# Batch normalization on one core: the first tile in one transfer, the four parameters as single rows from ScalarE's queue

## The chip, the core and the metric

The kernel runs on one core of a Trainium2 chip. The time is the device time of one execution in microseconds, from the program's start to its end; a kernel is run several times and the median is given. Beside it stands a profiled execution, from which all views below come.

## What is computed

```python
def reference(x, gamma, beta, running_mean, running_var):
    eps = 1e-5
    mean = running_mean.reshape(1, -1, 1, 1)
    ...
    return gamma * (x - mean) / np.sqrt(var + eps) + beta
```

`x` is 32 x 256 x 128 x 128 float32, 537 MB, and so is the output; the four parameters have 256 values each, one for each channel. Each value of `x` is multiplied by its channel's scale `gamma / sqrt(var + eps)`, and the channel's shift `beta - mean * scale` is added.

## The kernel before

**Tiles.** The 256 channels are two blocks of 128, one channel on each of the 128 partitions. One image and one block make a tile of 128 x 16384 values, 64 KB on each partition and 8.4 MB in all. There are 64 tiles (`NT`), and three buffers of that size (`NBUF`): tile `i` lies in buffer `i % 3`, is computed in place, and is stored from there.

**Loads (SP's queue).** The loop at L98 to L106 issues all loads in order of the tiles. The loads of tiles 1 and 2 wait for nothing. From tile 3 on, load `i` waits for two things: that the store of tile `i - 3`, which had the same buffer, has landed (L103), and that VectorE has done the first part of tile `i - 1` (L106), so that a load is issued just after the one before it has landed.

**The computation.** VectorE does a tile in two `tensor_scalar` instructions, columns 0 to 2560 and 2560 to 14336 (L160 to L162, through `vector_part`); the first of them waits for the tile's load. ScalarE does the last 2048 columns with one `activation` (`scalar_part`). The last tile is cut otherwise: ScalarE takes 7168 columns of it.

**Stores (ScalarE's queue).** In the loop at L163 to L168, ScalarE waits until both of VectorE's parts of tile `i` are done and until the store of tile `i - 1` has landed, does its own columns, and issues the store of the tile (`store`, L156). So there is at most one store under way at a time, and, from tile 3 on, at most one load.

**The start.** Tile 0 is an exception: it is loaded in two halves of 8192 columns, the left one at L90 with a semaphore of its own (`early`), the right one at L97. Between them stand the four parameters (L92 to L96), on the same queue. Each is read 16 times (`partition_broadcast(NE)`), 16 rows of 1 KB, into partitions 0 to 15 of a 32 x 1024 tile `rows`, which VectorE has set to zero before (L91); the first of the four transfers waits for that. All four count up one semaphore, `fetched`.

VectorE waits for `fetched`, transposes `rows` in blocks of 32 x 32 (L110), and copies the first column of each block to where it belongs (L115, four copies), so that each parameter then stands with one value on each partition. Only row 0 of `rows` is used by this. One square root on ScalarE (L117) and four small VectorE instructions (L124 to L127) make scale and shift. VectorE then does tile 0 in two parts, columns 0 to 8192 after `early` (L158) and 8192 to 14336 after the right half (L159).

Of the kernel before, what the change touches and what calls it, by code (L numbers as in the profile page):

```python
# [13 lines left out]
VCOLS = 14336  # L14
# [3 lines left out]
@with_exitstack  # L18
def kernel(
    ctx: ExitStack,  # L20
    tc: tile.TileContext,
    x: bass.AP,
    gamma: bass.AP,
    beta: bass.AP,
    running_mean: bass.AP,
    running_var: bass.AP,
    out: bass.AP,
):
    nc = tc.nc
    eps = 1e-5  # L30
    f32 = mybir.dt.float32

    N, C, H, W = x.shape
    P = nc.NUM_PARTITIONS
    assert C % P == 0
    NCB = C // P
    HW = H * W
    NT = N * NCB
    B = 32
    NQ = P // B  # L40
    NE = 16
    NPAR = 4

    xr = x.rearrange("n (cb p) h w -> (n cb) p (h w)", p=P)
    outr = out.rearrange("n (cb p) h w -> (n cb) p (h w)", p=P)

    params = ctx.enter_context(tc.tile_pool(name="params", bufs=1))
    data = ctx.enter_context(tc.tile_pool(name="data", bufs=1))
    params.tile([P, PAD], f32, name="pad", tag="pad")
    bufs = [data.tile([P, HW], f32, name=f"t{s}", tag=f"t{s}") for s in range(NBUF)]  # L50
    rows = params.tile([B, NPAR * C], f32, name="rows", tag="rows")
    turned = params.tile([B, NPAR * C], f32, name="turned", tag="turned")
    par = params.tile([P, NPAR, NCB], f32, name="par", tag="par")
    eps_t = params.tile([P, 1], f32, name="eps_t", tag="eps")
    std_t = params.tile([P, NCB], f32, name="std_t", tag="std")
    rstd_t = params.tile([P, NCB], f32, name="rstd_t", tag="rstd")
    scale_t = params.tile([P, NCB], f32, name="scale_t", tag="scale")
    ms_t = params.tile([P, NCB], f32, name="ms_t", tag="ms")
    shift_t = params.tile([P, NCB], f32, name="shift_t", tag="shift")

    loaded = [tc.alloc_semaphore(f"loaded{s}") for s in range(NBUF)]
    stored = [tc.alloc_semaphore(f"stored{s}") for s in range(NBUF)]
    early = tc.alloc_semaphore("early")
    vdone = tc.alloc_semaphore("vdone")
    adone = tc.alloc_semaphore("adone")
    fetched = tc.alloc_semaphore("fetched")
    vec = tc.alloc_semaphore("vec")
    act = tc.alloc_semaphore("act")  # L70

    with tc.tile_critical():  # L72
        count = [0]

        def step(inst, sem=None, value=None):

            if sem is not None:
                inst._wait_ge(sem, value)
            elif count[0]:
                inst._wait_ge(vec, count[0])  # L80
            inst.then_inc(vec, 1)
            count[0] += 1
            return count[0]

        left, right = slice(0, HW // 2), slice(HW // 2, HW)
        last = NT - 1

        nc.sync.dma_start(out=bufs[0][:, left], in_=xr[0][:, left]).then_inc(early, 16)  # L90
        zeroed = step(nc.vector.memset(rows[:], 0.0))  # L91
        for r, ap in enumerate((running_var, gamma, beta, running_mean)):  # L92
            inst = nc.sync.dma_start(out=rows[0:NE, r * C : (r + 1) * C], in_=ap.partition_broadcast(NE))  # L93
            if r == 0:
                inst._wait_ge(vec, zeroed)
            inst.then_inc(fetched, 16)  # L96
        nc.sync.dma_start(out=bufs[0][:, right], in_=xr[0][:, right]).then_inc(loaded[0], 16)  # L97
        for i in range(1, NT):  # L98
            s, turn = i % NBUF, i // NBUF


            if turn:
                nc.sync.wait_ge(stored[s], 16 * turn)  # L103
            inst = nc.sync.dma_start(out=bufs[s][:], in_=xr[i]).then_inc(loaded[s], 16)
            if turn:
                inst._wait_ge(vdone, 2 * (i - 1) + 1)  # L106


        step(nc.vector.memset(eps_t[:], eps))  # L109
        step(nc.vector.transpose(out=turned[:], in_=rows[:]), fetched, 16 * NPAR)  # L110

        blocks = turned.rearrange("p (rc q b) -> p rc q b", q=NQ, b=B)
        flat = par.rearrange("p r cb -> p (r cb)")
        for q in range(NQ):
            placed = step(nc.vector.tensor_copy(out=flat[q * B : (q + 1) * B], in_=blocks[:, :, q, 0]))  # L115
        var_t, gamma_t, beta_t, mean_t = (par[:, r] for r in range(NPAR))
        nc.scalar.activation(  # L117
            out=std_t[:],
            in_=var_t,
            func=mybir.ActivationFunctionType.Sqrt,  # L120
            bias=eps_t[:],
            scale=1.0,
        )._wait_ge(vec, placed).then_inc(act, 1)
        step(nc.vector.reciprocal(out=rstd_t[:], in_=std_t[:]), act, 1)  # L124
        step(nc.vector.tensor_mul(out=scale_t[:], in0=gamma_t, in1=rstd_t[:]))  # L125
        step(nc.vector.tensor_mul(out=ms_t[:], in0=mean_t, in1=scale_t[:]))  # L126
        ready = step(nc.vector.tensor_sub(out=shift_t[:], in0=beta_t, in1=ms_t[:]))  # L127
        nc.vector.wait_ge(vec, ready)

        def vector_part(i, first, end):  # L130
            t, cb = bufs[i % NBUF], i % NCB
            return nc.vector.tensor_scalar(  # L132
                out=t[:, first:end],
                in0=t[:, first:end],
                scalar1=scale_t[:, cb : cb + 1],
                scalar2=shift_t[:, cb : cb + 1],
                op0=mybir.AluOpType.mult,
                op1=mybir.AluOpType.add,
            ).then_inc(vdone, 1)

        def scalar_part(i, first):
            t, cb = bufs[i % NBUF], i % NCB
            return nc.scalar.activation(  # L143
                out=t[:, first:],
                in_=t[:, first:],
                func=mybir.ActivationFunctionType.Identity,
                bias=shift_t[:, cb : cb + 1],
                scale=scale_t[:, cb : cb + 1],
            ).then_inc(adone, 1)

        def landed(i):
            return loaded[i % NBUF], 16 * (i // NBUF + 1)

        def store(i):
            s = i % NBUF
            nc.scalar.dma_start(out=outr[i], in_=bufs[s][:])._wait_ge(adone, i + 1).then_inc(stored[s], 16)  # L156

        vector_part(0, 0, HW // 2)._wait_ge(early, 16)  # L158
        vector_part(0, HW // 2, VCOLS)._wait_ge(*landed(0))  # L159
        for i in range(1, NT):  # L160
            vector_part(i, 0, STEP)._wait_ge(*landed(i))
            vector_part(i, STEP, VLAST if i == last else VCOLS)  # L162
        for i in range(last):  # L163
            nc.scalar.wait_ge(vdone, 2 * (i + 1))
            inst = scalar_part(i, VCOLS)
            if i:
                inst._wait_ge(stored[(i - 1) % NBUF], 16 * ((i - 1) // NBUF + 1))
            store(i)  # L168
        scalar_part(last, VLAST)._wait_ge(*landed(last))
        nc.scalar.wait_ge(vdone, 2 * NT)  # L170
        store(last)

        for s in range(NBUF):
            nc.sync.wait_ge(stored[s], 16 * ((NT - s + NBUF - 1) // NBUF))
# [30 lines left out]
```

## Time and profile before

| | |
|---|---|
| median of the runs | 2482.92 us (2482.25 to 2483.06, 3 runs) |
| the profiled execution's own time | 2482.82 us |
| its span, first to last instruction | 2481.0 us |
| bytes moved by the DMA engines | 1073.85 MB, mean 433 GB/s |
| tile 1's landing, tile 2's, tile 3's | 55.57, 86.96, 125.66 us |
| store 0's landing, store 1's, store 2's | 72.42, 111.11, 149.79 us |
| last load's landing, last store's issue | 2446.04, 2452.43 us |

A landing is read here as the start of the instruction that waited for it: VectorE's first part for a load, ScalarE's `activation` for the store before.

The profile counts an engine as busy only while it computes. In the timelines, a line is the start, the duration, the engine, the line of the code and the operation with what it writes and reads; an engine's name with a q behind it (SPq, ACTq) is its sequencer, which here issues transfers. In brackets is the idle time before, and what ended it.

The core has 16 DMA engines, which all queues share. A transfer of 128 rows is spread over all 16, eight rows on each. Below the views, the trace keeps a record of each descriptor's data and of each semaphore write: its start, its duration, its size and its queue. Converted to the span's clock, these are the records of one DMA engine around the landing of tile 2 (86.96) and that of store 1 (111.11):

| start, us | what | us |
|---|---|---|
| 81.60 | row of load 2, its last | 2.42 |
| 84.01 | row of store 1 | 2.42 |
| 86.42 | load 2's semaphore write | 0.01 |
| 86.43, 88.84, 91.26 | three rows of store 1 | 2.42 each |
| 93.67 | row of load 3, its first | 2.42 |
| ... | rows of store 1 and load 3 in turn | 2.42 each |
| 105.74 | row of store 1, its last | 2.42 |
| 108.16 | row of load 3 | 2.42 |
| 110.57 | store 1's semaphore write | 0.01 |
| 110.58, 112.99, 115.40 | three rows of load 3 | 2.42 each |
| 117.82 | row of store 2, its first | 2.42 |

### The profile page before, as it was taken

The page shows a single profiled execution, that of the slowest core. Times are in us where ns is not written, and L with a number is a line of the kernel's source. Part 1 is how long each engine was busy: PE and PEld are TensorE (multiplying, and loading weights), DVE is VectorE, ACT ScalarE, POOL GpSimd, SP SyncE. Part 2 cuts the span into 40 slices and gives each one's busy share as a digit, 9 for nine tenths or more (in the row PEclk, how much of TensorE's full clock was granted, in tenths as well). Part 3 has the DMA queues.
Part 4 walks back from the last instruction along what each step waited for, and adds up shares of the span by engine and source line. Part 5 has one row for each costly group of instructions (what it writes and reads, how often), then busy time and mean ns, then how long its engine had stood idle before and what let it go on. Part 6 is the DMA issues. An engine that isn't in the chain of part 4 may idle for free.

```text
span 2481.0 us, 516 instructions
## 1 busy us (share of the span) xinstructions
DVE 508.8 (21%) x139; ACT 139.8 (6%) x66; POOL 0.2 (0%) x4
## 2 busy tenths in 40 slices
DVE  2122121221212212122121221212212122121120
ACT  0000000000000000000000000000000000000001
POOL 0000000000000000000000000000000000000000
DMA  9999999999999999999999999999999999999999
GB/s 411 435 440 428 433 440 432 430 440 432 430 440 437 427 438 436 428 437 436 432 433 438 430 434 437 432 432 437 434 431 436 437 428 437 437 428 435 437 432 402
DMA packets 18708, 1073.85 MB, mean 433 GB/s; under 512 B 2128, under 2 KB 2192, under 8 KB 2192
## 3 DMA queue, kind: packets, MB, share of 16 engines
q1 hardware_dynamic: 9488, 536.94, 50.0%
q10 hardware_dynamic: 9216, 536.88, 49.9%
q14 instruction: 4, 0.03, 0.0%
HBM read 536.94 MB, written 536.87 MB: 433 GB/s over the span
## 4 chain that ended last, share of the span: by engine, by line
DMA 92%; DVE 4%; another core or an unknown queue 2%; ACT 0%; issue 0%; SPq 0%; DVEq 0%
DMA t<-in_x_dram 92%; DVE t L132 4%; ACT t L143 0%; SPq L93 0%; DVE rows L91 0%; DVE eps_t L109 0%; DVEq L200 0%; SPq L72 0%
## 5 line engine op out<-in xcount | busy, mean ns | idle before, releaser
L132 DVE TENSOR_SCALAR t<-t,scale_t,shift_t 128x11776 f32<-128x11776 f32 (+2 forms) x128 | 505.3, 3989 | 1928.8 <-DMA t<-in_x_dram 1928.7
L143 ACT ACTIVATE t<-t,shift_t,scale_t 128x2048 f32<-128x2048 f32 x64 | 138.2, 2159 | 2297.8 <-DMA out_dram<-t 2274.9
L110 DVE STREAM_TRANSPOSE turned<-rows 32x1024 f32<-32x1024 f32 x1 | 1.2, 1232 | 11.8 <-DMA rows<-in_running_mean_dram 11.8
L117 ACT ACT_TABLE_LOAD x1 | 1.3, 1283 | 0.9 <-SPq L72 0.9
L91 DVE MEMSET rows<- 32x1024 f32 x1 | 0.9, 912 | 1.2 <-SPq L72 1.2
L117 ACT ACTIVATE std_t<-par,eps_t 128x2 f32<-128x2 f32 x1 | 0.3, 295 | 14.0 <-DVE par L115 14.0
L115 DVE COPY par<-turned 32x8 f32<-32x8 f32 x4 | 0.6, 162 | 0.1
L124 DVE RECIPROCAL rstd_t<-std_t 128x2 f32<-128x2 f32 x1 | 0.2, 166 | 0.4 <-ACT std_t L117 0.4
L125 DVE TENSOR_TENSOR scale_t<-par,rstd_t 128x2 f32<-128x2 f32 x1 | 0.2, 162 | 0.0
L127 DVE TENSOR_TENSOR shift_t<-par,ms_t 128x2 f32<-128x2 f32 x1 | 0.2, 162 | 0.0
L126 DVE TENSOR_TENSOR ms_t<-par,scale_t 128x2 f32<-128x2 f32 x1 | 0.2, 160 | 0.0
L189 POOL MEMSET const-bfloat16-1.0<- 128x1 bf16 x1 | 0.1, 101 | 0.0
L189 POOL MEMSET const-uint8-127<- 128x1 uint8 x1 | 0.1, 101 | 0.0
L189 POOL MEMSET const-float32-0.0<- 128x1 f32 x1 | 0.1, 98 | 0.2 <-issue 0.2
L189 POOL MEMSET const-float32-1.0<- 128x1 f32 x1 | 0.1, 98 | 0.0
L109 DVE MEMSET eps_t<- 128x1 f32 x1 | 0.1, 59 | 0.1
## 6 DMA issues: line engine op xcount, KB each, us to landing
t<-in_x_dram SPq DMA_DIRECT2D x2, 4096.0 KB, 15.9
out_dram<-t ACTq DMA_DIRECT2D x64, 36.5
t<-in_x_dram SPq DMA_DIRECT2D x63, 37.0
rows<-in_running_var_dram SPq DMA_DIRECT2D x1, 16.0 KB, 11.1
rows<-in_gamma_dram SPq DMA_DIRECT2D x1, 16.0 KB, 10.9
rows<-in_beta_dram SPq DMA_DIRECT2D x1, 16.0 KB, 10.7
rows<-in_running_mean_dram SPq DMA_DIRECT2D x1, 16.0 KB, 10.6
```

What stands on the lines that cost most here:

```text
L91: zeroed = step(nc.vector.memset(rows[:], 0.0))
L109: step(nc.vector.memset(eps_t[:], eps))
L110: step(nc.vector.transpose(out=turned[:], in_=rows[:]), fetched, 16 * NPAR)
L115: placed = step(nc.vector.tensor_copy(out=flat[q * B : (q + 1) * B], in_=blocks[:, :, q, 0]))
L117: nc.scalar.activation(out=std_t[:], in_=var_t, func=mybir.ActivationFunctionType.Sqrt, bias=eps_t[:], scale=1.0,)._wait_ge(vec, placed).t ...
L124: step(nc.vector.reciprocal(out=rstd_t[:], in_=std_t[:]), act, 1)
L125: step(nc.vector.tensor_mul(out=scale_t[:], in0=gamma_t, in1=rstd_t[:]))
L126: step(nc.vector.tensor_mul(out=ms_t[:], in0=mean_t, in1=scale_t[:]))
L127: ready = step(nc.vector.tensor_sub(out=shift_t[:], in0=beta_t, in1=ms_t[:]))
L132: return nc.vector.tensor_scalar(out=t[:, first:end], in0=t[:, first:end], scalar1=scale_t[:, cb : cb + 1], scalar2=shift_t[:, cb : cb + 1 ...
L143: return nc.scalar.activation(out=t[:, first:], in_=t[:, first:], func=mybir.ActivationFunctionType.Identity, bias=shift_t[:, cb : cb + 1] ...
L189: nc = _bacc.Bacc("TRN2", target_bir_lowering=False, num_devices=1)
```

## The change

Tile 0 is loaded like all others, in one transfer, by the same loop, and computed in the same two parts as all others; the semaphore `early` is gone. The four parameters are issued by ScalarE's queue instead of SP's, and each is read once, as one row of 1 KB into partition 0 of `rows`. The first of them still waits for the memset of `rows`. In ScalarE's order the four issues stand ahead of the table load for the square root.

```diff
-        nc.sync.dma_start(out=bufs[0][:, left], in_=xr[0][:, left]).then_inc(early, 16)
         zeroed = step(nc.vector.memset(rows[:], 0.0))
         for r, ap in enumerate((running_var, gamma, beta, running_mean)):
-            inst = nc.sync.dma_start(out=rows[0:NE, r * C : (r + 1) * C], in_=ap.partition_broadcast(NE))
+            inst = nc.scalar.dma_start(out=rows[0:1, r * C : (r + 1) * C], in_=ap.partition_broadcast(1))
             if r == 0:
                 inst._wait_ge(vec, zeroed)
             inst.then_inc(fetched, 16)
-        nc.sync.dma_start(out=bufs[0][:, right], in_=xr[0][:, right]).then_inc(loaded[0], 16)
-        for i in range(1, NT):
+        for i in range(NT):
             s, turn = i % NBUF, i // NBUF
...
-        vector_part(0, 0, HW // 2)._wait_ge(early, 16)
-        vector_part(0, HW // 2, VCOLS)._wait_ge(*landed(0))
-        for i in range(1, NT):
+        for i in range(NT):
             vector_part(i, 0, STEP)._wait_ge(*landed(i))
             vector_part(i, STEP, VLAST if i == last else VCOLS)
```

More of the change, by code (lines that the diff above doesn't have):

```diff
@@ L40 @@
     NQ = P // B
-    NE = 16
     NPAR = 4
@@ L64 @@
     stored = [tc.alloc_semaphore(f"stored{s}") for s in range(NBUF)]
-    early = tc.alloc_semaphore("early")
     vdone = tc.alloc_semaphore("vdone")
@@ L83, in step @@
             return count[0]
-        left, right = slice(0, HW // 2), slice(HW // 2, HW)
         last = NT - 1
-        nc.sync.dma_start(out=bufs[0][:, left], in_=xr[0][:, left]).then_inc(early, 16)
         zeroed = step(nc.vector.memset(rows[:], 0.0))
         for r, ap in enumerate((running_var, gamma, beta, running_mean)):
-            inst = nc.sync.dma_start(out=rows[0:NE, r * C : (r + 1) * C], in_=ap.partition_broadcast(NE))
+            inst = nc.scalar.dma_start(out=rows[0:1, r * C : (r + 1) * C], in_=ap.partition_broadcast(1))
             if r == 0:
```

## The prediction

> **What bounds the kernel now.** I read the page's share of busy time and its slices first, then its queue table, then the timelines of the start and of one steady tile.
>
> ```profile
> span 2481.0 us, 516 instructions
> DVE 508.8 (21%) x139; ACT 139.8 (6%) x66; POOL 0.2 (0%) x4
> DMA  9999999999999999999999999999999999999999
> q1 hardware_dynamic: 9488, 536.94, 50.0%
> q10 hardware_dynamic: 9216, 536.88, 49.9%
> ```
>
> DVE and ACT are nearly idle; the 16 DMA engines are busy in every slice, half for the loads (q1, SP's queue), half for the stores (q10, ScalarE's). A store has 9216/64 = 144 packets: 128 rows of 64 KB, eight on each engine, and 16 semaphore writes. One row costs an engine 0.499 x 2481.0 / (64 x 8) = 2.418 us; I call that a slot. 1024 slots fill 2476 of 2481.0 us. Two things follow: almost nothing can be gained, and whatever leaves the DMA engines without work is lost in full.
>
> ```profile
> 86.96 7.93 DVE L132 TENSOR_SCALAR t<-t,scale_t,shift_t 128x2560 f32<-128x2560 f32 x2 [23.45 <-DMA t<-in_x_dram]
> 88.60 39.02 SPq L104 DMA_DIRECT2D t<-in_x_dram  x2
> 111.11 2.09 ACT L143 ACTIVATE t<-t,shift_t,scale_t 128x2048 f32<-128x2048 f32 x1 [36.60 <-DMA out_dram<-t]
> 113.24 0.34 ACTq L156 DMA_DIRECT2D out_dram<-t  x1
> 125.66 7.93 DVE L132 TENSOR_SCALAR t<-t,scale_t,shift_t 128x2560 f32<-128x2560 f32 x2 [30.76 <-DMA t<-in_x_dram]
> 149.79 2.09 ACT L143 ACTIVATE t<-t,shift_t,scale_t 128x2048 f32<-128x2048 f32 x1 [36.59 <-DMA out_dram<-t]
> ```
>
> A load lands at 125.66 (DVE starts), a store at 149.79 (ACT starts), one tile after the store at 111.11: period 38.68 = 16 slots, eight loaded and eight stored rows. Each queue has a hole in every period: a load is issued 1.64 after the last one landed (86.96 to 88.60), a store 2.13 after the last one (111.11 to 113.24). These holes cost nothing only because the two queues' ends lie 24.1 us (10 slots) apart, so that the other queue's rows fill them. That distance is 24.15 here and 24.63 near the end (2406.90 to 2431.53): nothing restores it, it is what the start made of it. So the question is what the change does to it.
>
> **The rule by which the engines share.** The trace's packet records (put on the span's clock, by taking the landing writes as the landings) show it for one engine: last load row to 84.01, a store row to 86.42, then the load's semaphore write, then three store rows in the hole, then load rows again. Each queue gets one descriptor per turn, and a semaphore write is a turn of its own. The next turn is chosen when the running row starts: at the first store, issued at 29.06, engines whose load row started at 30.50 or before took another load row, those from 30.63 on a store row. So a DMA becomes eligible some 1.53 us after its issue begins.
>
> **The change, part by part.**
>
> ```profile
> 0.95 0.37 SPq L90 DMA_DIRECT2D t<-in_x_dram  x1
> 2.16 0.34 SPq L93 DMA_DIRECT2D rows<-in_running_var_dram  x1
> 14.10 1.23 DVE L110 STREAM_TRANSPOSE turned<-rows 32x1024 f32<-32x1024 f32 x1 [11.85 <-DMA rows<-in_running_mean_dram]
> 17.35 4.55 DVE L132 TENSOR_SCALAR t<-t,scale_t,shift_t 128x8192 f32<-128x8192 f32 x1
> 26.94 2.09 ACT L143 ACTIVATE t<-t,shift_t,scale_t 128x2048 f32<-128x2048 f32 x1 [10.49 <-DVE t L132]
> 29.06 0.38 ACTq L156 DMA_DIRECT2D out_dram<-t  x1
> ```
>
> *The parameters.* In one queue with the tile's left half they arrive right behind it: 14.10. Now ScalarE's queue carries four DMAs, issued at about 2.16, 2.55, 3.00 and 3.47 as SP's were (the first waits for the memset, ended at 2.13). Behind them on ScalarE stand the table load (1.28) and the square root, which needs the parameters anyway: no cost. Four data descriptors and four semaphore writes are eight turns, each behind one 64 KB row of load 0. The first rows start at 2.3 to 3.1 us, before 2.16+1.53 = 3.7, so the first parameter follows row 1 or 2. After row 1, the eighth item follows row 8; after row 2, seven rows and the load's own short semaphore write come between: the same moment. So the parameters land together with all of load 0, whether one row of 1 KB goes to one engine or is cut over all of them. Load 0 landed at 23.43 with some 0.5 us of parameters inside; I take 22.9, and the parameters land at 22.9 instead of 14.1.
>
> The Trainium skill ("DMA: Bandwidth & Descriptors", section "Queues, rings and completion order") says that an engine drains a whole packet, typically 9 to 17 descriptors, from one queue before it switches. By that rule the eight items would need one turn or two, the parameters would be there by about 10 us, and the time would be that of the first rival. The records above show a single semaphore write waiting a full row, so I go by them.
>
> *The first tile.* With both there at 22.9: transpose to first TENSOR_SCALAR 17.35-14.10 = 3.25, the tile's two vector parts 7.93 (any other tile's row; 4.55+3.48 before), ScalarE's part and issue 0.03+2.09+0.03. Store 0 is issued at 22.9+3.25+7.93+2.15 = 36.2 instead of 29.06. That in itself costs nothing: loads 1 and 2 keep the engines full (24 rows, 58 us). SP's five fewer instructions bring loads 1 and 2 out 3 us sooner (4.41 before), behind a queue that is full anyway: nothing. The 64 parameter descriptors saved, about 0.5 us, are a gain of the same size at most.
>
> *What is late next: the distance.* Store 0 is eligible at 36.2+1.53 = 37.7. Row 9 of the loads starts at 22.3 to 22.9 (the engines lie 0.5 to 0.7 apart), row 15 six slots later at 36.8 to 37.4, too early; row 16 at 39.2 to 39.8. So a store row comes first after 16 load rows (before: (30.6-23.1)/2.418, after 12 or 13). Then turns alternate from 41.6 to 42.2: S1, load 1's semaphore write, S2, L17, S3, L18 and so on to S8, L23, store 0's write, L24, load 2's write. Store 0 lands after 15 slots, at 78.5, and load 2 after 16, at 80.9. The ends are one slot apart instead of ten.
>
> From there both holes fall together. Store 1 is issued at 78.5+0.05+2.13 = 80.7; the last load row ends at 80.9, and nothing is eligible. The price of such a hole: landing to issue 2.18, issue to running 2.41 (at the very start, issue 0.95, the last engine ended its first 32 KB row of 1.21 at 4.57), less the one row that still ran, 2.42: 2.17 us. Bounds: 2.13+1.35-2.42 = 1.06 where the row runs after 1.35 (the earliest engine then) without a slow first row; 2.77 with a first row stretched by 1.3, as the longest at the first store was (3.71 for 2.42), in place of 0.7. I take 2.1, near the start's row, since that is the only idle start that the trace has.
>
> It repeats. Load 3 is issued at 80.95+1.64 = 82.6, eligible at 84.1, after store 1's first row has chosen its second. Then S1 S2 L1 S3 ... S8 L7, store's write, L8, load's write: again one slot between the ends, and again the hole, for stores 1 to 62. Sum: 62 x 2.1 = 130, on the profiled execution's 2482.82 (span 2481.0 and 1.8 around it, 0.1 below the runs' median 2482.92): 2613. Bounds: 62 x 1.06 = 66 gives 2549, 62 x 2.77 = 172 gives 2655.
>
> **The rivals.** *No change, 2482.* If the eight items pass in few turns, the parameters are early and DVE waits for load 0 at 22.9: store 0 issued at 22.9+7.93+2.15 = 33.0, eligible at 34.5, so after 14 load rows: ends some 14 slots apart, holes filled. 2482.8 less 0.5. It decides from parameters before about 19.6 (22.9-3.25), and holds up to about one slot later, 22. For it: only the load's big rows have been seen taking turns. Against: the semaphore write that waited. This is the case on the other side: not slower.
>
> *The coincidence doesn't last.* A row delayed on one engine (the records have some up to 0.7 us) pushes the ends apart after some tens of tiles. Half the tiles: 2482.8+65 = 2548. Against it: an idle start brings the 16 engines back into step each period.
>
> *Load first.* One turn more for the parameters, say 25.3: seven load rows are left, load 2 ends first, and the hole is the load's: 1.69+2.41-2.42 = 1.68 and the store's remaining wait. 62 x 1.68 = 104 at least: 2587, inside the forecast's range.
>
> *A real gain* is excluded beyond the slack 2481.0-2476 = 5 us, most of it the start's and the end's latency.
>
> **How the numbers follow.** Coincidence through the whole run (load or store first) 0.80; one that breaks 0.03; no change 0.16; a gain over 0.2% (5 us, about what such a measurement can tell from no change) 0.01. Range 2540 to 2655: the bounds above, the lower a little wider; it leaves out no change and some of the broken coincidences, 0.2 in all. Slower 0.83, same 0.16, faster 0.01.
>
> **What would show it.** Transpose at about 23 instead of 14.1; first TENSOR_SCALAR at 26.2; first store issued at 36.2; DVE's tiles 40.7 apart instead of 38.7; the DMA share near 0.95 in every stretch; a store landing about 2.4 before a load, each period. A transpose before 19 makes the prediction wrong at its first step; landings ten or more us apart with a late transpose, at the count of rows; the coincidence with another period, at the price of the hole.

## The result, and the profile after

The changed kernel takes 2598.87 us (2591.43 to 2602.3, 5 runs) where the one before takes 2482.92 (2481.96 to 2484.78, 5 runs beside it): 1.0464 times as long, 95% interval 1.0447 to 1.0481. (Times are medians; ratios compare the means of the runs, so they can differ in the last digit from the ratio of the medians.) The profiled execution has a span of 2589.7 us, 108.7 more than before.

From the page of the changed kernel, the span, the slices and the queues:

```profile
span 2589.7 us, 515 instructions
DMA  9999999999999999999999999999999999999999
GB/s 415 403 428 403 423 406 421 413 406 396 421 411 431 405 425 410 424 409 421 413 422 412 421 405 421 421 416 392 423 405 421 421 421 405 421 421 412 430 405 405
q10 hardware_dynamic: 9224, 536.88, 49.8%
q1 hardware_dynamic: 9216, 536.88, 49.1%
rows<-in_running_var_dram ACTq DMA_DIRECT2D x1, 1.0 KB
```

The same tiles move at a lower rate all through the run, 415 GB/s on average instead of 433: this is no loss at the start alone, every stretch pays. Yet the two queues' rows occupy the engines for 98.9% of a longer span. Most of the added time stands inside rows. ScalarE's queue has 9224 packets, eight more than 64 stores: each parameter is one packet of 1 KB and one semaphore write, all on one engine.

The timeline of the start, and of three tiles later on:

```profile
2.15 0.52 ACTq L87 DMA_DIRECT2D rows<-in_running_var_dram  x1
22.75 1.23 DVE L103 STREAM_TRANSPOSE turned<-rows 32x1024 f32<-32x1024 f32 x1 [20.50 <-DMA rows<-in_running_mean_dram]
26.00 7.94 DVE L125 TENSOR_SCALAR t<-t,scale_t,shift_t 128x2560 f32<-128x2560 f32 x2
36.09 0.37 ACTq L149 DMA_DIRECT2D out_dram<-t  x1
79.92 2.09 ACT L136 ACTIVATE t<-t,shift_t,scale_t 128x2048 f32<-128x2048 f32 x1 [43.86 <-DMA out_dram<-t]
82.33 7.93 DVE L125 TENSOR_SCALAR t<-t,scale_t,shift_t 128x2560 f32<-128x2560 f32 x2 [28.35 <-DMA t<-in_x_dram]
...
730.10 2.09 ACT L136 ACTIVATE t<-t,shift_t,scale_t 128x2048 f32<-128x2048 f32 x1 [39.60 <-DMA out_dram<-t]
732.87 7.93 DVE L125 TENSOR_SCALAR t<-t,scale_t,shift_t 128x2560 f32<-128x2560 f32 x2 [31.70 <-DMA t<-in_x_dram]
734.51 81.55 SPq L97 DMA_DIRECT2D t<-in_x_dram  x3
769.90 2.09 ACT L136 ACTIVATE t<-t,shift_t,scale_t 128x2048 f32<-128x2048 f32 x1 [37.70 <-DMA out_dram<-t]
774.73 7.94 DVE L125 TENSOR_SCALAR t<-t,scale_t,shift_t 128x2560 f32<-128x2560 f32 x2 [33.93 <-DMA t<-in_x_dram]
809.27 2.09 ACT L136 ACTIVATE t<-t,shift_t,scale_t 128x2048 f32<-128x2048 f32 x1 [37.29 <-DMA out_dram<-t]
814.09 7.93 DVE L125 TENSOR_SCALAR t<-t,scale_t,shift_t 128x2560 f32<-128x2560 f32 x2 [31.42 <-DMA t<-in_x_dram]
```

The parameters arrive at 22.75 instead of 14.10, the first store is issued at 36.09 instead of 29.06, and store 0 and load 2 land 2.41 us apart (79.92 and 82.33; 72.42 and 86.96 before). Later a store lands 2.77 before a load (730.10, 732.87), the next one 4.83 (769.90, 774.73), the one after 4.82 (809.27, 814.09), and the loads are 41.86 and 39.36 apart, where they were 38.64. So landings a slot or two apart persist to the end: by the records, two slots or a little more in 44 of 62 tiles, less in the others.

The packet records tell what a period pays. At two slots' distance the store's next row is eligible only while the load's last row already runs; that first row then takes 3.1 to 3.5 us instead of 2.42, and the period is some 39.5. At one slot the engine idles some 1.3 first; the store's first row then takes 2.45, but the store row that runs just ahead of the load's first row takes about 3.1 and that load row about 3.4: some 42. Summed over the run, as a mean of the 16 engines (a row's excess is over 2.415):

| kernel | engines idle, us | excess in rows, us | landing that comes first, distance in mid-run |
|---|---|---|---|
| before | 0 | 5.4 | ten slots apart |
| changed | 27.1 | 86.2 | store, 2.4 to 4.8 us |
| e11_late5 | 27.7 | 92.5 | store, 2.4 to 4.8 us |
| e7_nowait | 140.4 | 102.7 | load, 2.4 us |
| e5_late12 | 132.0 | 106.1 | load, 2.4 us |
| e12_short_hole | 18.6 | 73.5 | load, 4.8 to 9.8 us |
| e13_split0 | 0 | 5.8 | ten slots apart |

For the changed kernel 27.1 + 86.2 - 5.4 = 108 us, against 108.7 between the spans. The split is good to some 3 us: records of one engine overlap by a few ns, and if that is not subtracted the idle time is some 30 us.

### The profile page after: what moved, and what is told of

It is laid out like the page before. It is cut to its first block, busy times and chain, and to the rows that moved or that the text cites. A ratio compares the mean times of both kernels' runs of the same rounds, so it can differ in the third digit from the quotient of the medians.

```text
span 2589.7 us, 515 instructions
## 1 busy us (share of the span) xinstructions
DVE 508.7 (20%) x139; ACT 139.8 (5%) x66; POOL 0.2 (0%) x4
## 3 DMA queue, kind: packets, MB, share of 16 engines
q10 hardware_dynamic: 9224, 536.88, 49.8%
## 4 chain that ended last, share of the span: by engine, by line
DMA 93%; DVE 4%; another core or an unknown queue 1%; ACT 0%; issue 0%; SPq 0%
DMA t<-in_x_dram 93%; DVE t L125 4%; ACT t L136 0%; SPq L97 0%; SPq L191 0%; SPq L70 0%
## 5 line engine op out<-in xcount | busy, mean ns | idle before, releaser
L125 DVE TENSOR_SCALAR t<-t,scale_t,shift_t 128x2560 f32<-128x2560 f32 (+1 forms) x128 | 505.2, 3989 | 2023.8 <-DMA t<-in_x_dram 2023.7
```

The source lines that it names most:

```text
L125: return nc.vector.tensor_scalar(out=t[:, first:end], in0=t[:, first:end], scalar1=scale_t[:, cb : cb + 1], scalar2=shift_t[:, cb : cb + 1 ...
```

## The experiments

Every kernel here was measured beside the kernel before on the same chip; ratios are to that, whose medians were 2483.42 to 2484.58.

**One half of the change at a time.** First the parameters alone:

```diff
-            inst = nc.sync.dma_start(out=rows[0:NE, r * C : (r + 1) * C], in_=ap.partition_broadcast(NE))
+            inst = nc.scalar.dma_start(out=rows[0:1, r * C : (r + 1) * C], in_=ap.partition_broadcast(1))
```

> Only the parameters are moved (single rows, ScalarE's queue); tile 0 keeps its two halves. Theory (turns behind big rows, then the distance between the two queues' ends): each of the eight turns now stands behind a row of 32 KB, 1.21 us instead of 2.42, so the transpose begins at 13 to 14.5 us, store 0 is issued at 28 to 30, a load and a store land 8 to 12 slots apart, 2480 to 2485 us. Rival (ScalarE's queue or the one-row transfers themselves cost the 116 us): 2590 to 2605.

Measured: 2483.63, ratio 0.9998 (0.9989 to 1.0008). The transpose begins at 14.14, the first store is issued at 28.30, store 1 lands 24.45 after load 2. ScalarE's queue and single rows cost nothing by themselves.

Then the first tile alone, with the parameters on SP's queue behind it:

```diff
             inst = nc.sync.dma_start(out=bufs[s][:], in_=xr[i]).then_inc(loaded[s], 16)
+            if i == 0:
+                for r, ap in enumerate((running_var, gamma, beta, running_mean)):
+                    fetch = nc.sync.dma_start(out=rows[0:16, r * C : (r + 1) * C], in_=ap.partition_broadcast(16))
...
```

> Only the first tile is changed (one transfer); the parameters are again 16 rows each on SP's queue, behind tile 0. Theory: they arrive behind load 0, transpose at about 23, store 0 issued at about 36, landings one or two slots apart, 2585 to 2615 us, though no parameter goes through ScalarE's queue. Rival (the single rows or ScalarE's queue are the cause): 2480 to 2490.

Measured: 2595.89 to 2607.10 in three executions, ratio 1.0479 (1.0457 to 1.0501). No parameter went through ScalarE's queue, and the loss is there, as the theory has it. The fourth execution took 2736.70 us, at the same granted clock of 1.00, and the ratio leaves it out; it is the one with the profile. There the transpose starts at 24.29 and the first store is issued at 37.62, load 2 lands 0.17 before store 0 (87.70, 87.87), and from then on the load stays first. So this kernel starts at a tie that can fall either way; e5_late12 reaches that order on purpose. The three others have no trace, so that their landings are as the theory says is argued from their times.

**Only the first store late.** Copies of finished columns into a spare tile, ahead of store 0 alone, in the kernel before:

```diff
+            if i == 0:
+                for k in range(7):
+                    copy = nc.scalar.activation(out=pad[:], in_=bufs[i % NBUF][:, 0:PAD], ...)
...
             store(i)
```

> The kernel before, with seven copies of 936 columns on ScalarE ahead of store 0 alone, some 1.2 us each, 8.4 in all; nothing else is changed, and the parameters arrive at 14.1 as before. The copies add nothing to the output. Theory: store 0 issued at about 37.5, as late as in the changed kernel, and all else follows from it: landings one or two slots apart to the end, 2585 to 2630 us. Rival (a late start costs its own delay once): 2483 to 2492.

Measured: 2601.56, ratio 1.0475 (1.0459 to 1.049). Its start, in the timeline:

```profile
14.04 1.23 DVE L111 STREAM_TRANSPOSE turned<-rows 32x1024 f32<-32x1024 f32 x1 [11.79 <-DMA rows<-in_running_mean_dram]
28.98 8.35 ACT L171 ACTIVATE pad<-t,shift_t,scale_t 128x936 f32<-128x936 f32 x7
37.42 0.38 ACTq L157 DMA_DIRECT2D out_dram<-t  x1
79.84 2.09 ACT L144 ACTIVATE t<-t,shift_t,scale_t 128x2048 f32<-128x2048 f32 x1 [42.51 <-DMA out_dram<-t]
82.30 7.94 DVE L133 TENSOR_SCALAR t<-t,scale_t,shift_t 128x2560 f32<-128x2560 f32 x2 [28.46 <-DMA t<-in_x_dram]
```

Parameters and first tile are those of before, the store is 8.4 us late, and store 0 and load 2 land 2.46 apart, as in the changed kernel. 8.4 us of delay cost some 118. The other sizes:

> As e3_late7 with three copies, 3.6 us. Theory: store 0 issued at about 32.7 and eligible at 34.2, after 14 load rows instead of 12 or 13; a load and the next store land 11 to 14 slots apart instead of ten, still far from 16, every hole is filled: 2481 to 2486 us, not a part of the 119 us of the seven copies. Rival (the loss grows with the delay): 3.6/8.4 of it, about 2534.

> As e3_late7 with five copies, 6.0 us: store 0 issued at 34.9, eligible at 36.5, after 15 load rows on every DMA engine; store 0 lands at about 76 and load 2 at about 81, two slots apart. New theory (e8_quarters lost the full price though its store 0 came at 32.95: two slots apart are already too few, and the price is rows that take longer, not engines that idle): 2590 to 2610. The prediction's step (holes are filled at two slots apart, and only one slot or none is lost): 2481 to 2487.

> As e3_late7 with twelve copies, 14.4 us: store 0 issued at 43.3, after load 1 has landed, so that load 2 ends first and load 3 has to wait for store 0. Theory (which of the two lands first sets the price): the load lands before the store, as in e7_nowait, period about 42.4, 2700 to 2745. The prediction's price for load first: 2587 or a little over.

| delay of store 0, us | store 0 issued | load rows ahead of it | us | ratio, 95% interval |
|---|---|---|---|---|
| 0 (before) | 29.06 | 12 or 13 | 2482.92 | 1 |
| 3.6 (e4_late3) | 32.50 | 14 | 2485.42 | 1.0005 (0.9995 to 1.0014) |
| 6.0 (e11_late5) | 34.87 | 15 | 2598.62 | 1.0431 (1.0373 to 1.0489) |
| 8.4 (e3_late7) | 37.42 | 16 | 2601.56 | 1.0475 (1.0459 to 1.049) |
| 14.4 (e5_late12) | 43.43 | 18 or 19 | 2718.06 | 1.0945 (1.0929 to 1.0961) |

A staircase, not a slope: nothing at 3.6, nearly all of it at 6.0 (one of its four executions took 2567.56, the others 2598.25 to 2599.13), and a second step, twice as high, where the load lands first. At 3.6, landings are 29.0 us (twelve slots) apart and four slots from the next one; there the holes are still filled. The 6.0 us speak against the prediction, which had no loss at two slots' distance.

**Early parameters.** The changed kernel, with tile 0 in four transfers of 16 KB rows (VectorE waits for all four):

```diff
+            if i == 0:
+                for k in range(4):
+                    part = slice(k * HW // 4, (k + 1) * HW // 4)
+                    nc.sync.dma_start(out=bufs[0][:, part], in_=xr[0][:, part]).then_inc(loaded[0] if k == 3 else early, 16)
+                continue
```

> The changed kernel, with tile 0 loaded in four quarters of 16 KB rows; VectorE still waits for all four, the parameters still come as single rows through ScalarE's queue. Theory: a turn behind a row of 16 KB is 0.6 us, so the transpose begins at 8 to 11 us, scale and shift wait for the tile, store 0 is issued at 32 to 34, landings 11 to 14 slots apart: 2480 to 2486. Rival (ScalarE's queue, or waiting for the whole tile 0, is the cause): 2590 to 2610.

Measured: 2596.83, ratio 1.0453 (1.0436 to 1.047). The timeline:

```profile
10.09 1.23 DVE L109 STREAM_TRANSPOSE turned<-rows 32x1024 f32<-32x1024 f32 x1 [7.84 <-DMA rows<-in_running_mean_dram]
22.85 7.94 DVE L131 TENSOR_SCALAR t<-t,scale_t,shift_t 128x2560 f32<-128x2560 f32 x2 [9.63 <-DMA t<-in_x_dram]
32.95 0.37 ACTq L155 DMA_DIRECT2D out_dram<-t  x1
77.76 2.09 ACT L142 ACTIVATE t<-t,shift_t,scale_t 128x2048 f32<-128x2048 f32 x1 [44.84 <-DMA out_dram<-t]
82.59 7.93 DVE L131 TENSOR_SCALAR t<-t,scale_t,shift_t 128x2560 f32<-128x2560 f32 x2 [24.08 <-DMA t<-in_x_dram]
```

The turns are right: behind rows a quarter as long, the same eight descriptors are there at 10.09 instead of 22.75. The time expected is wrong. Store 0 is issued at 32.95, hardly later than the 32.50 of e4_late3, but with no parameters in the loads' queue the rows of load 1 begin 0.5 us earlier (22.3 to 22.9, against 22.8 to 23.3), and on three engines a 15th load row goes first; store 0 and load 2 land 4.83 apart. Waiting for the whole tile 0 is thus enough for the full loss, however early the parameters are.

The same kernel, with tile 0 shared between VectorE and ScalarE as the last tile is:

> As e8_quarters, with tile 0 cut between VectorE and ScalarE as the last tile is (9216 and 7168 columns at once), so that store 0 is issued at 22.85+6.4 = 29.2 instead of 32.95. Theory: eligible at 30.8, after 13 load rows; landings five slots apart or more, 2480 to 2486, with the first tile whole and the parameters on ScalarE's queue. Rival (waiting for the whole first tile costs by itself): 2590 to 2605.

```diff
-            vector_part(i, STEP, VLAST if i == last else VCOLS)
+            vector_part(i, STEP, VLAST if i in (0, last) else VCOLS)
...
+            if i == 0:
+                nc.scalar.wait_ge(vec, ready)
+                nc.scalar.wait_ge(early, 48)
+                scalar_part(0, VLAST)._wait_ge(*landed(0))
...
```

Measured: 2482.77, ratio 0.9998 (0.9989 to 1.0008).

```profile
29.13 0.38 ACTq L155 DMA_DIRECT2D out_dram<-t  x1
87.03 7.94 DVE L131 TENSOR_SCALAR t<-t,scale_t,shift_t 128x2560 f32<-128x2560 f32 x2 [25.87 <-DMA t<-in_x_dram]
111.16 2.09 ACT L142 ACTIVATE t<-t,shift_t,scale_t 128x2048 f32<-128x2048 f32 x1 [36.59 <-DMA out_dram<-t]
```

Store 0 is issued at 29.13, store 1 lands 24.13 after load 2. Waiting for the whole tile costs nothing if the store still goes out in time.

**Moving the ends apart later.** The changed kernel, with a single load that waits for VectorE's second part too:

```diff
-                inst._wait_ge(vdone, 2 * (i - 1) + 1)
+                inst._wait_ge(vdone, 2 * (i - 1) + (2 if i == 3 else 1))
```

> The changed kernel, with one wait longer: load 3 alone waits until VectorE has done both parts of tile 2, not the first one, so it is issued 6.3 us later. Theory: that one delay takes the two queues' ends 5 slots or more apart, and the holes are filled from then on: 2483 to 2492 us. Rival (whatever is slow in the changed kernel is renewed in every tile): 2590 to 2610.

Measured: 2488.59, ratio 1.0021 (1.0012 to 1.0031): one wait of 6.3 us saves 110, and some 5 us of the loss stay.

```profile
82.97 7.94 DVE L125 TENSOR_SCALAR t<-t,scale_t,shift_t 128x2560 f32<-128x2560 f32 x2 [29.14 <-DMA t<-in_x_dram]
90.93 0.33 SPq L97 DMA_DIRECT2D t<-in_x_dram  x1
```

Load 3 is issued 7.96 after load 2 has landed instead of 1.64. By the records, store 1 lands 32.5 after load 2, and from then on, up to the last tile, a store lands 24.15 to 24.54 after a load, as before.

> As e9_wait3, but it is load 32 that waits for both of VectorE's parts, once, in mid-run. Theory: the changed kernel's period of 40 to 42 us up to load 32, 38.6 after it: half of the loss, 2535 to 2555 us. Rival (only the first tiles decide, and what e9_wait3 mended was the start): 2590 to 2610.

Measured: 2541.44, ratio 1.0233 (1.0218 to 1.0248), half of the loss. Two stretches of its profile (length, busy time of VectorE, ScalarE and GpSimd, clock, DMA share, GB/s):

```profile
500.00:1000.00 500.00, 95.22 (x24) 25.11 (x12) 0.00 (x0) 1.00 0.99 413
1500.00:2000.00 500.00, 103.15 (x26) 27.20 (x13) 0.00 (x0) 1.00 1.00 434
```

413 GB/s ahead of tile 32, 434 behind it, in one execution with one start. What is slow is the relation of the two queues, and it was changed at tile 3 as well as at tile 32.

**The wait that keeps the distance.** The kernel before, without L105 and L106:

```diff
-            if turn:
-                inst._wait_ge(vdone, 2 * (i - 1) + 1)
```

> The kernel before, without the wait of the loads for VectorE (L106); they still wait for the store of the tile that had their buffer, which is the only one that the data needs. Theory: the loads' queue then has no hole, gains on the stores in each period, until each load waits for a store's landing; then load and store are issued after the same landing and their holes coincide: 2590 to 2745 us, with the parameters and the first tile untouched. Rival (the wait is a cost or nothing): 2478 to 2486.

Measured: 2721.52, ratio 1.0959 (1.0943 to 1.0976). One period:

```profile
1184.49 7.93 DVE L130 TENSOR_SCALAR t<-t,scale_t,shift_t 128x2560 f32<-128x2560 f32 x2 [34.16 <-DMA t<-in_x_dram]
1186.90 43.30 SPq L104 DMA_DIRECT2D t<-in_x_dram  x2
1186.91 2.09 ACT L141 ACTIVATE t<-t,shift_t,scale_t 128x2048 f32<-128x2048 f32 x1 [40.03 <-DMA out_dram<-t]
1189.03 0.34 ACTq L154 DMA_DIRECT2D out_dram<-t  x1
1227.48 7.93 DVE L130 TENSOR_SCALAR t<-t,scale_t,shift_t 128x2560 f32<-128x2560 f32 x2 [35.05 <-DMA t<-in_x_dram]
```

The issue of the load and ScalarE's part now start at the same landing, a store's (1186.90, 1186.91); the load before had landed 2.4 us earlier (1184.49), but the buffer came free only then. The period is 42.99 here. A wait that no data needs was worth some 237 us.

**A shorter hole.** The changed kernel, with ScalarE doing 256 columns from tile 2 on:

> The changed kernel, with ScalarE doing 256 columns instead of 2048 from tile 2 on (VectorE does the rest, some 1 us more for each tile): a store is issued 0.65 after a landing instead of 2.13, so it is eligible 2.2 after it, inside one slot. Theory (the price is paid where a queue's next row is not eligible when the row ahead of it starts): the stores' hole has no price any more, and as it is shorter than the loads', the stores gain until the ends are far apart: 2482 to 2530. Rival (the price comes from both queues ending near each other, whatever the hole): 2585 to 2610.

Measured: 2565.53, ratio 1.0321 (1.0304 to 1.0338), neither. The stores' rows have 2.8 us of excess left of 51.7, as the theory has it, but the price is still paid: some 28 of the loads' 70.7 us of excess are in rows that run just ahead of a store's first row, and some 21 in the loads' own first rows. With holes of unequal length the distance moves from tile to tile: by the records, the first landings of loads and stores are 37.5, 29.0, 25.0 and 20.2 us apart, so the ends pass the good distance of before and run on to 4.8 to 9.8, with the load first. There the stores' hole is not short any more: ScalarE waits for VectorE's second part, not for the store before, in 33 tiles (1294.2 us in all), since VectorE's 8.87 us for a tile begin only when its load lands. So this run does not tell what a short hole alone would do; it shows that unequal holes do not keep their distance.

## Why the prediction was right, and where it wasn't

*The turns.* Right, to a fraction of a microsecond: eight items, one behind each row, on one engine. The records have the four parameters at 7.9, 12.8, 17.6 and 22.5 us, two slots each. The Trainium skill's rule of whole packets ("DMA: Bandwidth & Descriptors", "Queues, rings and completion order"), by which the prediction estimated them there by about 10, does not describe what these two queues did: behind 64 KB rows they took until 22.75, behind 16 KB rows until 10.09.

*The start.* Transpose, first TENSOR_SCALAR and first store were put at 23, 26.2 and 36.2, and came at 22.75, 26.00 and 36.09. By the records exactly 16 load rows ran on every engine before the first store row, as counted. Store 0 and load 2 were put at 78.5 and 80.9, and came at 79.92 and 82.33: the order and the distance hold, both 1.4 late, since the load rows that ran just ahead of the first store's rows took 3.6 to 3.9 us. (Two readings of the start before are not exact. Of the four load rows that began at 30.63 to 30.68, three were followed by a store row and one by another load row, so 1.53 us from issue to eligible holds for most engines, not all. And the row of 3.71 us was no first row, but a load row ahead of a store's first row, which took 2.42.)

*It repeats.* Shown by the distances in the trace to the end of the run, and by e9_wait3 and e10_wait32, which end it. But the ends are not one slot apart each time: they are two slots apart in 44 of 62 tiles, with periods of some 42 and 39.5. VectorE's tiles are 40.4 us apart on average, where 40.7 was named.

*The price.* The term that was mis-sized: 2.1 us for each store, 130 in all, against (2598.87 - 2482.92)/62 = 1.87 and 116. Its make-up was wrong. The prediction had some 1.4 us of idle engines and 0.7 of a slow first row in each hole; it was 27.1/62 = 0.44 idle and 80.8/62 = 1.30 in slow rows, of both queues. So the DMA share stayed at 0.99, where 0.95 was named as the sign. That the two errors nearly cancel, and the sum comes out 14 us high, is luck.

*The rival of no change.* Its condition was wrong: it was to hold with parameters before 19.6 to 22 us. e8_quarters had them at 10.09 and lost all of it, and e11_late5 lost it at the same distance with the old parameters. The prediction counted two slots' distance as filled, because it priced a hole at the time without an eligible row; rows around a late start are slow too, though no engine idles. So the late parameters were not needed for the loss: waiting for the whole tile was enough. The forecast had the right answer with one condition too many, and the 0.16 that it gave to no change rested on a case that is slow as well.

*Load first.* Put at 2587 or a little over, inside the range, it is 2718 (e5_late12) and 2722 (e7_nowait), beyond the range: both queues then wait for the same landing, and the engines idle for 132 to 140 us. The prediction had the store ahead by one slot alone, and in the five runs of the changed kernel it stayed ahead; that it would was counted rightly, but narrowly, as the fourth execution of e2_whole_behind shows.

*A real gain* was excluded by the full DMA engines, and e1_halves_rows and e13_split0, with the single rows and all waits for the tile paid in time, are at 0.9998 of the kernel before.

## What to carry to other kernels

Where two queues share full DMA engines and each has a hole between its transfers, what counts is when the holes come, not how long the start takes: look at the distance of the two queues' landings in one steady tile before shifting anything at the start, and keep the landings several rows apart (with the store first and holes of three rows, four were enough here, two were not; three were not tried). A transfer of a few small descriptors on a queue of its own did not overtake big rows here; each of its descriptors, and each semaphore write, waited for one of them. And a wait that no data needs may be what holds two queues apart.

## What was not expected of the hardware

Where a transfer starts late, rows take longer though no engine idles: the DMA share of 0.99 hides 81 of the 108 us. Two kinds of rows are long. One is a transfer's first row: at two slots' distance the store's first row takes 3.1 to 3.5 us instead of 2.42, and it became eligible only after the row ahead of it had started. The other is the row that runs just ahead of the other queue's first row: the load rows of 3.6 to 3.9 us ahead of the changed kernel's first store, and in e7_nowait every load's second row, with some 57 us in all. That lateness alone is the cause is not shown: in the changed kernel the load issued at 734.51 was, by the same 1.53 us, eligible at 736.0; the store rows ahead of it began at 738.3 and 738.4 on two engines, and yet its first rows behind them took 2.95 and 4.34. Why these rows are long, and none is in the steady tiles of before, stays open; no run separated the reading of descriptors from the reading of data. With unequal holes the two queues' ends drift (e12_short_hole), with equal ones (three slots each, before) a store lands 24.15 us after a load in all but a few of some 60 tiles, and after one at 25.26 it is back at 24.15 in the next.
